# Loading the first input ahead of the key weights, and one burst for the second modulation

## The chip, the cores and the metric

The kernel runs on one core of a Trainium2 chip. The metric is device time in microseconds of one execution, the median of several runs. In the profile PE is TensorE's matmul side and PEld its weight loads, DVE is VectorE, ACT is ScalarE, POOL is GpSimd, and SP is SyncE, whose queue issues nearly all DMAs here.

## What is computed

Two post-norm layers run over 1024 latent tokens and 256 context tokens of width 1024. Each layer modulates its input with a shift and a scale made from a conditioning vector, projects it to queries, keys, values and a gate, attends (windowed attention with 16 query heads over 4 key heads in the first layer, neighbourhood attention in the second), gates, projects back and normalises. The part that matters here is the very start of layer one:

```python
shift, scale, gate = jnp.split(silu_c @ w_ada[i] + b_ada[i], 3, axis=-1)
shift_c, scale_c, gate_c = jnp.split(silu_cc @ w_ada[i] + b_ada[i], 3, axis=-1)
u = h * (1.0 + scale[:, None, :]) + shift[:, None, :]
uc = hc * (1.0 + scale_c) + shift_c
...
q, k, v, g = _split_a(u @ w_in)
```

## The kernel before

The width of 1024 is cut into eight slices of 128 rows, called kt. Tokens stand in the free dimension: 1280 of them, in chunks (CHUNKS) of 512, 512 and 256; the first two are latent tokens, the last is the context.

Products are made at high precision from two parts: a tile is copied by ACT to a rounded high part (L164 for weights, wh; L568 for inputs, uAh), and the difference from the original, made by DVE or POOL, is the low part (L166, wl; L569, uAl). One product is three matmuls: high by high, low weight by high input, high weight by low input (L578, L579, L580 for keys; L588 to L590 for values).

The first stage is a loop over kt from -1 to 8 (L594). Its pieces:

- `mod_load(kt)` (L518) issues DMAs: two tiles of modulation weights (wada, 512 KB each), the weights of the key and value projections that are due (wr, 256 KB each, by `w.load`), and the slice of the input (hraw, 640 KB, 1280 tokens).
- `mod_rows(kt)` (L527) multiplies the conditioning vectors with the modulation weights: 16 calls, 32 matmul instructions, into one half of the PSUM tile kc. For kt above 1 these stand in one burst: each call after the first is tied to the call emitted just before it on TensorE (`keep_in_program_order`). For kt 0 and 1 they are free, so that each half can run when its weights are there. ACT copies the result to rows (L544).
- `mod(kt)` (L546) sums the rows with one small matmul (L549) whose moving operand is sel, the last four columns of the tile bad, and adds the biases, other columns of bad, on DVE (L550). The result adc holds shift and scale.
- `u_make(kt)` (L557) applies scale and shift to the three chunks in place (ACT at L564 for the first chunk, DVE at L566 for the other two), and makes high and low parts.
- `k_mm(kt)` (L571) makes the key products of the slice, into kp for the latent tokens (512 wide) and kc for the context (256 wide), for two halves of the key columns (nt). `v_mm(kt)` (L582) makes the value products of the first 512 tokens.
- `w.split(n)` (L153) makes high and low parts of the weight tiles up to number n. Tiles 0, 1, 4 and 5 are key weights, 2, 3, 6 and 7 value weights.

Before the loop, 12 bf16 matmuls on zeros run (L475), and 12 more after the first modulation (L607).

What each engine does in what order is not the order of the text. A planner sets it when the program is built: it goes by the order of emission and by when it reckons that operands are ready, and then fixes one order for each engine; at run time each engine goes through its list strictly. DMAs are issued by SP in one such list. The tile bad is loaded second of all, behind cT, the conditioning vectors.

Of the kernel before, what the change touches and what calls it, by code (L numbers as in the profile page):

```python
# [15 lines left out]
ALU = mybir.AluOpType  # L16
# [14 lines left out]
CHUNKS = ((0, 512), (512, 512), (1024, 256))  # L31
# [12 lines left out]
def f32(ap):  # L44
    return ap.bitcast(F32)
# [37 lines left out]
def build(tc, i, out):  # L83
    nc = tc.nc
    mm = nc.tensor.matmul
    dma = nc.sync.dma_start
# [18 lines left out]
    cT = cp.tile([P, KT, 2], F32, name="cT")  # L105
    dma(cT, i["cT"])
    bad = cp.tile([P, 52], F32, name="bad")
    dma(bad, i["bada"])
    sel = bad[:, 48:52]
    lnc = cp.tile([P, 2, KT], F32, name="lnc")  # L110
    half = cp.tile([P, 1], F32, name="half")
# [25 lines left out]
    class Weights:  # L137
# [15 lines left out]
        def split(self, upto):  # L153
            while self.ns < min(upto, self.cap):
                j = self.ns
                self.load(j + 1)
                r = self.raw.pop(j)
                if j in VALUES:
                    t = pp.tile([P, 2, 512], F32R, tag="wada", bufs=10, name=f"wv{j}")
                    hi, lo = t[:, 0], t[:, 1]  # L160
                else:
                    hi = wp.tile([P, 512], F32R, tag="whi", bufs=4, name=f"wh{j}")
                    lo = wp.tile([P, 512], F32R, tag="wlo", bufs=4, name=f"wl{j}")
                nc.scalar.copy(hi, r)  # L164
                e = nc.vector if j < 8 or j >= NA and j % 2 else nc.gpsimd
                e.tensor_tensor(lo, r, f32(hi), ALU.subtract)  # L166
                self.got[j] = (hi, lo)
                self.ns += 1
# [14 lines left out]
    NA = len(srcs)  # L183
# [6 lines left out]
    w = Weights(srcs)  # L190
# [280 lines left out]
    def warm(out, n):  # L471
        for _ in range(n):
            mm(out, zero[:, 0:P], zero, start=True, stop=True)
# [2 lines left out]
    nc.scalar.activation(th0, cT, AF.Tanh, scale=0.5)  # L476
    nc.vector.scalar_tensor_tensor(th0, th0, 1.0, cT, ALU.add, ALU.mult)
    nc.vector.tensor_scalar(sil[:, :, 0:2], th0, 0.5, None, ALU.mult)
    nc.vector.tensor_scalar(bad[:, 8:16], bad[:, 8:16], 1.0, None, ALU.add)
    cos = ap_.tile([P, S], F32, name="cos")  # L480
    sin = ap_.tile([P, S], F32, name="sin")
    msk = ap_.tile([P, 1152], BF16, name="msk")
# [33 lines left out]
    raws, wada, rows = {}, {}, {}  # L516

    def mod_load(kt, upto):  # L518

        wada[kt] = [pp.tile([P, 4, 2 * P], F32, tag="wada", bufs=10, name="wada") for _ in range(2)]  # L520
        for hf in range(2):
            dma(wada[kt][hf], i["wadaC"][kt, hf])
        w.load(upto)
        raws[kt] = pp.tile([P, T], F32, tag="hraw", bufs=4, name="hraw")
        dma(raws[kt], i["hT"][:, kt, :])

    def mod_rows(kt):  # L527

        ws = wada.pop(kt)

        burst = kt > 1
        for n, hf in enumerate((1, 0) if burst else (0, 1)):
            for r in range(2):
                for x in range(2):
                    for kh in range(2):
                        g = 32 * (2 * x + kh)
                        ins = mm(
                            kc[g : g + 32, 512:640], sil[:, 4 * hf + 2 * r + kh, :], ws[hf][:, 2 * r + kh, x * P : (x + 1) * P],
                            start=n + r == 0, stop=n + r == 2, tile_position=(0, g),
                        )  # L540
                        if burst and n + r + x + kh:
                            tc.keep_in_program_order(ins)
        rows[kt] = pp.tile([P, P], F32, tag="rows", bufs=2, name="rows")
        nc.scalar.copy(rows[kt], kc[:, 512:640])  # L544

    def mod(kt):  # L546

        pa = kc[:, 768 + 4 * kt : 772 + 4 * kt]
        mm(pa, rows.pop(kt), sel, start=True, stop=True)  # L549
        nc.vector.tensor_tensor(  # L550
            adc[:, kt],
            pa.rearrange("p (x v) -> p x v", x=2),
            bad[:, kt : kt + 9 : 8].unsqueeze(2).to_broadcast([P, 2, 2]),
            ALU.add,
        )

    def u_make(kt):  # L557
        r = raws.pop(kt)
        for c, (t0, n) in enumerate(CHUNKS):
            v, tok = c // 2, slice(t0, t0 + n)  # L560
            x = r[:, tok]
            sc, sh = adc[:, kt, 1, v : v + 1], adc[:, kt, 0, v : v + 1]
            if c == 0:
                nc.scalar.activation(x, x, AF.Identity, bias=sh, scale=sc)  # L564
            else:
                nc.vector.tensor_scalar(x, x, sc, sh, ALU.mult, ALU.add)  # L566
            hi, lo = uA.at(kt, tok)
            nc.scalar.copy(hi, x)  # L568
            nc.vector.tensor_tensor(lo, x, f32(hi), ALU.subtract)  # L569

    def k_mm(kt):  # L571
        for c, (t0, n) in enumerate(CHUNKS):
            for nt in range(2):
                hi, lo = w.got[KEYS[2 * (kt // 4) + nt]]
                sl = slice((kt % 4) * P, (kt % 4 + 1) * P)
                rh, rl = uA.at(kt, slice(t0, t0 + n))
                pt = kps[c, nt] if c < 2 else kc[:, nt * C : nt * C + C]
                mm(pt, hi[:, sl], rh, start=kt == 0 and (c < 2 or nt == 0), stop=False)  # L578
                mm(pt, lo[:, sl], rh, start=False, stop=False)  # L579
                mm(pt, hi[:, sl], rl, start=False, stop=kt == KT - 1 and (c < 2 or nt == 1))  # L580

    def v_mm(kt):  # L582
        hi, lo = w.got[VALUES[kt // 2]]
        sl = slice((kt % 2) * 256, (kt % 2 + 1) * 256)
        for t in range(4):
            lh, ll = uA.at(kt, slice(t * P, (t + 1) * P))
            pt = vps[:, t * 256 : (t + 1) * 256]
            mm(pt, lh, hi[:, sl], start=kt == 0 and t % 2 == 0, stop=False)  # L588
            mm(pt, lh, lo[:, sl], start=False, stop=False)
            mm(pt, ll, hi[:, sl], start=False, stop=kt == KT - 1 and t % 2 == 1)  # L590


    upto = (2, 3, 4, 4, 6, 7, 8, 8)
    for kt in range(-1, KT + 1):  # L594
        if kt + 1 < KT:
            for n in range(3) if kt < 0 else (kt + 3,) if kt + 3 < KT else ():
                mod_load(n, upto[n])
                if n == 0:
                    w.split(2)
            mod_rows(kt + 1)  # L600
        if kt > 0:
            k_mm(kt - 1)
        if kt + 1 < KT:
            mod(kt + 1)
        if kt < 0:

            warm(vps[:, 0:512], 12)  # L607
        if kt > 0:
            v_mm(kt - 1)
        if kt < KT and kt >= 0:  # L610
            u_make(kt)
            w.split(upto[min(kt + 1, 7)])
    dma(ident, i["ident"])
    dma(lnc, i["lnc"])
# [168 lines left out]
    def att_steps(subs, qk, st, tr, pv, last_of_unit, costs, need, ahead, rise, split=False):  # L783

        seq = []
        n = len(subs)
        for k in range(-ahead, n + 2 + split):
            row = []

# [51 lines left out]
    for p in range(8):  # L841
# [6 lines left out]
        if p < 7:  # L848
            n = len(att)
# [323 lines left out]
    for n, row in enumerate(rowsB):  # L1173
        ex = []
        if n < len(subsB):
            h, jp, r = subsB[n]
# [65 lines left out]
    for b in range(8):  # L1242
        x = ob.tile([P, D], F32, tag="x", bufs=3, name="x")
# [129 lines left out]
```

## Time and profile before

| | |
|---|---|
| median of 3 runs | 1434.9 us |
| lowest and highest run | 1433.47 and 1436.19 us |
| the profiled execution | 1432.09 us, of which the span is 1430.3 us |
| first matmul of the first modulation (L537) | 5.63 us |
| first input's modulation begins (L564, L566) | 10.02 us |
| first key product (L578) | 11.94 us |
| first keys taken from PSUM (L494) | 58.85 us |

The span runs from the first to the last instruction of the profile; all times within are microseconds from its start. A row of the timeline has start, duration, engine, line, operation, output and inputs, count, and in brackets the idle time just before with what ended it. Weight loads overlap matmuls and matmuls overlap each other, so the distance between two starts says more than a duration.

### The profile page before, as it was taken

The page shows a single profiled execution, that of the slowest core. Times are in us where ns is not written, and L with a number is a line of the kernel's source. Part 1 is how long each engine was busy: PE and PEld are TensorE (multiplying, and loading weights), DVE is VectorE, ACT ScalarE, POOL GpSimd, SP SyncE. Part 2 cuts the span into 40 slices and gives each one's busy share as a digit, 9 for nine tenths or more (in the row PEclk, how much of TensorE's full clock was granted, in tenths as well). Part 3 has the DMA queues.
Part 4 walks back from the last instruction along what each step waited for, and adds up shares of the span by engine and source line. Part 5 has one row for each costly group of instructions (what it writes and reads, how often), then busy time and mean ns, then how long its engine had stood idle before and what let it go on. Part 6 is the DMA issues. An engine that isn't in the chain of part 4 may idle for free. (4 is left out here: it accounts for less than half of the span.)

```text
span 1430.3 us, 25152 instructions
## 1 busy us (share of the span) xinstructions
PE 1388.8 (97%) x8816; PEld 1215.8 (85%) x8816; DVE 978.4 (68%) x2214; ACT 732.1 (51%) x1559; POOL 631.2 (44%) x779
## 2 busy tenths in 40 slices
PE   8999999999999999999999999999999999998997
PEld 6988898888888888788898899888988899887876
DVE  4658887878878789566433765555665665667598
ACT  4337776676776778332222545545454454557300
POOL 0326676667666667233311333333233233336663
PEclk9999999999999999999999999999999999999999
DMA  9572114123222123444287575464655464476564
GB/s 367 182 229 85 57 53 129 48 79 101 70 71 63 56 80 121 133 132 133 71 258 219 156 202 166 141 173 145 176 150 170 141 192 147 120 206 199 140 162 133
DMA packets 127453, 202.39 MB, mean 141 GB/s; under 512 B 9696, under 2 KB 65376, under 8 KB 127328
## 3 DMA queue, kind: packets, MB, share of 16 engines
q1 hardware_dynamic: 127328, 200.79, 47.0%
q8 instruction: 70, 1.15, 0.3%
q14 instruction: 55, 0.45, 0.1%
HBM read 145.18 MB, written 55.57 MB: 140 GB/s over the span
## 5 line engine op out<-in xcount | busy, mean ns | idle before, releaser
L332 POOL TENSOR_SCALAR s_B<-s_B,rs_B 128x640 f32<-128x640 f32 (+1 forms) x128 | 102.5, 801 | 294.1 <-DVE rs_B L331 250.4
L210 PE MATMUL pj<-uBh,wh 128*128 128x512 f32 (+1 forms) x448 | 175.9, 393 | 0.0
L211 PE MATMUL pj<-uBl,wh 128*128 128x512 f32 (+1 forms) x448 | 170.1, 380 | 0.0
L212 PE MATMUL pj<-uBh,wl 128*128 128x512 f32 (+1 forms) x448 | 170.1, 380 | 0.0
L327 ACT ACTIVATE s_B<-s_B,m_B 128x640 f32<-128x640 f32 (+1 forms) x128 | 102.9, 804 | 129.5 <-DVE m_B L320 128.9
L327 ACT ACTIVATE s_A<-s_A,m_A 128x641 f32<-128x641 f32 (+2 forms) x160 | 119.5, 747 | 81.9 <-DVE m_A L320 59.2
L166 POOL TENSOR_TENSOR wl<-wr,wh 128x512 fp32r<-128x512 f32 x64 | 87.4, 1365 | 159.5 <-ACT wh L164 145.5
L332 POOL TENSOR_SCALAR s_A<-s_A,rs_A 128x640 f32<-128x640 f32 (+2 forms) x160 | 129.6, 810 | 63.6 <-DVE rs_A L331 57.4
L320 DVE CUSTOM_DVE_ANT_0 s_A<-S_A,msk,nsk 128x640 f32<-128x640 f32 (+2 forms) x160 | 123.6, 774 | 31.2 <-PE S_A L735 16.2
L210 PE MATMUL pj<-uAh,wh 128*128 128x512 f32 (+1 forms) x384 | 140.1, 365 | 0.8 <-DVE otmp L774 0.8
L211 PE MATMUL pj<-uAl,wh 128*128 128x512 f32 (+1 forms) x384 | 137.6, 358 | 0.0
L345 DVE TENSOR_TENSOR pt_B<-T_B,pt_B 128x640 fp32r<-128x640 f32 (+1 forms) x128 | 100.9, 788 | 53.4 <-ACT pt_B L343 52.9
L212 PE MATMUL pj<-uAh,wl 128*128 128x512 f32 (+1 forms) x384 | 137.2, 357 | 0.0
L345 DVE TENSOR_TENSOR ptl_A<-T_A,pth_A 128x640 fp32r<-128x640 f32 (+2 forms) x160 | 114.2, 713 | 14.8 <-PE pvA L763 7.3
L339 PE MATMUL T_A<-ident,s_A 128*128 128x128 f32 x672 | 100.9, 275 | 10.6 <-DVE m_A L320 4.5
L339 PEld LDWEIGHTS T_A<-ident,s_A 128*128 128x128 f32 x672 | 77.3, 140 | 37.4 <-POOL s_A L332 10.1
L320 DVE CUSTOM_DVE_ANT_0 s_B<-S_B,bias 128x640 f32<-128x640 f32 (+1 forms) x128 | 100.3, 784 | 10.1 <-PE S_B L1067 9.3
L343 ACT CAST pt_B<-T_B 128x640 fp32r<-128x640 f32 (+1 forms) x128 | 84.5, 660 | 41.0 <-PE T_B L339 40.1
L343 ACT CAST pth_A<-T_A 128x640 fp32r<-128x640 f32 (+2 forms) x160 | 96.4, 602 | 16.5 <-PE T_A L339 15.1
L212 PEld LDWEIGHTS pj<-uBh,wl 128*128 128x128 f32 x448 | 84.2, 188 | 16.6
L339 PE MATMUL T_B<-ident,s_B 128*128 128x128 f32 x608 | 88.6, 275 | 8.8 <-DVE m_B L320 4.5
L339 PEld LDWEIGHTS T_B<-ident,s_B 128*128 128x128 f32 x608 | 70.3, 141 | 27.1 <-issue 13.5
(221 smaller groups left out, 3887.7 us busy)
## 6 DMA issues: line engine op xcount, KB each, us to landing
kB<-kdB SPq DMA_DIRECT2D x64, 320.0 KB, 5.2
gw<-in_wadaT SPq DMA_DIRECT2D x48, 256.0 KB, 2.8
vdB<-st SPq DMA_DIRECT2D x20, 512.0 KB, 3.5
vB<-vdB SPq DMA_DIRECT2D x16, 640.0 KB, 4.6
wada<-in_wadaC SPq DMA_DIRECT2D x16, 512.0 KB, 9.6
kdB<-st SPq DMA_DIRECT2D x16, 512.0 KB, 2.9
qdB<-st SPq DMA_DIRECT2D x16, 512.0 KB, 3.6
qB<-qdB SPq DMA_DIRECT2D x32, 256.0 KB, 4.7
```

The costliest lines, as they stand in the source:

```text
L166: e.tensor_tensor(lo, r, f32(hi), ALU.subtract)
L210: mm(pt[:, :n], hi[:, sl], rh, start=kt == 0, stop=False)
L211: mm(pt[:, :n], hi[:, sl], rl, start=False, stop=False)
L212: mm(pt[:, :n], lo[:, sl], rh, start=False, stop=kt == KT - 1)
L320: nc.vector.tensor_tensor_reduce(outp, sc, in1, scale, init if init is not None else 3e38, ALU.add, ALU.min, accum_out=s.m)
L327: nc.scalar.activation(s.t[:, :n], s.t[:, :n], AF.Exp, bias=s.m, scale=-1.0, accum_out=s.sum)
L332: nc.gpsimd.tensor_scalar(s.t[:, : s.w], s.t[:, : s.w], s.rs, 1.0, ALU.mult, ALU.mult)
L339: nc.tensor.transpose(tp[:, k * P : (k + 1) * P], s.t[:, src * P : (src + 1) * P], ident)
L343: nc.scalar.copy(pt.hi[:, :n, hl, :], tv)
L345: nc.vector.tensor_tensor(pt.lo[:, :n, hl, :], tv, f32(pt.hi[:, :n, hl, :]), ALU.subtract)
```

## The change

Four things change, all in the first stage.

1. The DMA of bad and the addition of 1 to its scale columns move from the head of the program into `mod_load(0)`, behind the first input.
2. In `mod_load(0)` the first input's DMA is issued ahead of the two key weights.
3. For kt = 0, `u_make` and `w.split(2)` move to the head of the iteration: the first chunk is modulated first (now on DVE), then the two key weights are split, then the other two chunks are modulated (the context on POOL). The ACT copies of the two key weights are tied to the instruction emitted before them on ACT, and the low part of the second one goes from DVE to POOL.
4. The first chunk's six key matmuls are emitted ahead of the second modulation. The second modulation (kt = 1) becomes one burst too, all its calls tied, the first one to the last of these key matmuls. The other two chunks' key products stay where all of them stood.

```diff
@@ head @@
-    dma(bad, i["bada"])
...
-                nc.scalar.copy(hi, r)
-                e = nc.vector if j < 8 or j >= NA and j % 2 else nc.gpsimd
+                ins = nc.scalar.copy(hi, r)
+                if j < 2:
+                    tc.keep_in_program_order(ins)
+                e = nc.vector if j < 8 and j != 1 or j >= NA and j % 2 else nc.gpsimd
...
-    nc.vector.tensor_scalar(bad[:, 8:16], bad[:, 8:16], 1.0, None, ALU.add)
...
-        w.load(upto)
         raws[kt] = pp.tile([P, T], F32, tag="hraw", bufs=4, name="hraw")
+        if kt:
+            w.load(upto)
         dma(raws[kt], i["hT"][:, kt, :])
+        if kt == 0:
+            dma(bad, i["bada"])
+            nc.vector.tensor_scalar(bad[:, 8:16], bad[:, 8:16], 1.0, None, ALU.add)
+            w.load(upto)
...
-        burst = kt > 1
+        burst = kt > 0
...
-                        if burst and n + r + x + kh:
+                        if kt == 1 or burst and n + r + x + kh:
                             tc.keep_in_program_order(ins)
...
-    def u_make(kt):
-        r = raws.pop(kt)
-        for c, (t0, n) in enumerate(CHUNKS):
+    def u_make(kt, cs=(0, 1, 2)):
+        r = raws[kt]
+        for c in cs:
+            t0, n = CHUNKS[c]
...
-            if c == 0:
+            if c == 0 and kt:
                 nc.scalar.activation(x, x, AF.Identity, bias=sh, scale=sc)
+            elif c == 2 and not kt:
+                nc.gpsimd.tensor_scalar(x, x, sc, sh, ALU.mult, ALU.add)
             else:
                 nc.vector.tensor_scalar(x, x, sc, sh, ALU.mult, ALU.add)
...
     for kt in range(-1, KT + 1):
+        if kt == 0:
+            u_make(0, (0,))
+            w.split(2)
+            u_make(0, (1, 2))
+            k_mm(0, (0,))
         if kt + 1 < KT:
             for n in range(3) if kt < 0 else (kt + 3,) if kt + 3 < KT else ():
                 mod_load(n, upto[n])
-                if n == 0:
-                    w.split(2)
             mod_rows(kt + 1)
         if kt > 0:
-            k_mm(kt - 1)
+            k_mm(kt - 1, (0, 1, 2) if kt > 1 else (1, 2))
...
-            u_make(kt)
+            if kt:
+                u_make(kt)
             w.split(upto[min(kt + 1, 7)])
```

More of the change, by code (lines that the diff above doesn't have):

```diff
@@ L569, in u_make, with k_mm @@
             nc.vector.tensor_tensor(lo, x, f32(hi), ALU.subtract)
-    def k_mm(kt):
-        for c, (t0, n) in enumerate(CHUNKS):
+    def k_mm(kt, cs=(0, 1, 2)):
+        for c in cs:
+            t0, n = CHUNKS[c]
             for nt in range(2):
```

## The prediction

> **What bounds the kernel now.** I read the page's head and busy times first, then the windows of the first stage (busy time of PE, PEld, DVE, ACT, POOL with counts, granted clock, DMA share, GB/s).
>
> ```profile
> span 1430.3 us, 25152 instructions
> PE 1388.8 (97%) x8816; PEld 1215.8 (85%) x8816; DVE 978.4 (68%) x2214; ACT 732.1 (51%) x1559; POOL 631.2 (44%) x779
> ...
> 24.00:36.00 12.00, 12.00 (x128) 10.36 (x128) 7.62 (x17) 6.40 (x13) 0.00 (x0) 1.00 1.03 405
> 57.00:80.00 23.00, 23.00 (x184) 22.52 (x183) 15.79 (x23) 4.99 (x10) 10.63 (x7) 1.00 0.47 160
> ```
>
> TensorE is busy 97% of the span, and the change touches only the first stage. From 24 to 36 us, and again from 57 to 80, PE has no gap, although the DMA engines are still full (share 1.03). So a microsecond won on PE before 24 us should reach the end, and what is not won there cannot be won later by this change. Which PE work stands at the start, and what releases it, is in the timeline of PE (start, duration, line, operation):
>
> ```profile
> 7.99 0.39 PE L549 MATMUL kc<-bad,rows 128*128 128x4 f32 x2
> 8.23 1.67 PE L473 MATMUL vps<-zero 128*128 128x512 bf16 x7
> 11.36 0.65 PE L537 MATMUL kc<-wada,sil 128*32 128x128 f32 x16 [1.46 <-DMA wada<-in_wadaC]
> 11.94 0.50 PE L578 MATMUL kp<-uAh,wh 128*128 128x512 f32 x1
> 13.37 0.65 PE L537 MATMUL kc<-wada,sil 128*32 128x128 f32 x16
> 13.94 0.50 PE L580 MATMUL kp<-uAl,wh 128*128 128x512 f32 x1
> 16.41 0.50 PE L578 MATMUL kp<-uAh,wh 128*128 128x512 f32 x1 [0.34 <-ACT uAh L568]
> 18.67 1.08 PE L537 MATMUL kc<-wada,sil 128*32 128x128 f32 x32
> 20.25 0.28 PE L578 MATMUL kc<-uAh,wh 128*128 128x256 f32 x1
> 20.96 0.28 PE L549 MATMUL kc<-bad,rows 128*128 128x4 f32 x2
> 22.75 0.39 PE L589 MATMUL vps<-wv,uAh 128*128 128x256 f32 x1 [1.06 <-DVE wv L166]
> ```
>
> Three idle stretches: 1.46 us before 11.36, 0.34 before 16.41, 1.06 before 22.75. They are all that PE can win besides doing the same work denser: 2.9 us of 1432. Pitches: the six 256-wide key products from 20.25 to 20.96 give 0.12 each, so 0.24 for a 512-wide one; half a modulation takes 0.57 (13.37 to 13.94), and one in a single burst about 1.0 (the 1.08 of the row at 18.67, less the overlap of the last). The context's six 256-wide products of the first input stand at 20.25, behind products of the second input: the order on an engine is not the text's but is fixed when the program is built.
>
> **The transfers.** Issue times from the timeline of SP, time to landing from the DMA view of the stretch around each issue (KB, us to landing):
>
> ```profile
> 1.19 0.42 SPq L108 DMA_DIRECT2D bad<-in_bada  x1
> bad<-in_bada SPq DMA_DIRECT2D x1, 26.0 KB, 2.1
> 2.12 0.43 SPq L522 DMA_DIRECT2D wada<-in_wadaC  x1
> wada<-in_wadaC SPq DMA_DIRECT2D x1, 512.0 KB, 4.6
> 3.07 0.43 SPq L150 DMA_DIRECT2D wr<-in_wAk  x1
> wr<-in_wAk SPq DMA_DIRECT2D x1, 256.0 KB, 5.3
> 3.54 0.43 SPq L525 DMA_DIRECT2D hraw<-in_hT  x1
> hraw<-in_hT SPq DMA_DIRECT2D x1, 640.0 KB, 6.4
> 5.71 0.59 SPq L525 DMA_DIRECT2D hraw<-in_hT  x1
> hraw<-in_hT SPq DMA_DIRECT2D x1, 640.0 KB, 9.0
> 4.50 0.51 SPq L522 DMA_DIRECT2D wada<-in_wadaC  x1
> wada<-in_wadaC SPq DMA_DIRECT2D x1, 512.0 KB, 8.0
> 7.75 0.33 SPq L522 DMA_DIRECT2D wada<-in_wadaC  x1
> wada<-in_wadaC SPq DMA_DIRECT2D x1, 512.0 KB, 10.6
> ```
>
> Landings are issue plus wait: bad 3.3, first modulation weights whole 6.7, second key weight 8.4, first input 9.9, second modulation weights whole 12.5, second input 14.7, third modulation weights 18.35. They come in the order of issue. From 8.4 to 9.9 the 640 KB of the input took 1.57 us, 0.41 MB/us.
>
> In the changed kernel bad leaves the front: one issue slot, 1.19 to 1.65, so the weights land at about 6.25. The input no longer has 512 KB of key weights ahead: 512/0.41 = 1.28 us. First input: 9.94 - 1.28 - 0.46 = **8.2**. The key weights land 0.64 and 1.28 us behind it, at 8.9 and 9.5. Bad lands between 4.7 (issue near 2.6 plus its 2.1) and 9.5 (with the key weights); I take 8.2, right behind the input, because all the quoted landings keep the order; at 9.5 all below would be 1.3 later, the sum +0.8. [...] Everything behind this group has the same bytes ahead as before: the second modulation's weights still land at 12.5, the second input at 14.7. SP's later issues wait for earlier landings, and the third modulation's may now wait for the input at 8.2 instead of the weights at 6.7. I cost that at nothing: the transfer of 7.75 took 10.6 us to land, so the engines have several microseconds queued; without that cover it would be up to 1.5 us on the third input.
>
> **The first products.** Rows for the chain:
>
> ```profile
> 3.36 0.17 DVE L479 TENSOR_SCALAR bad<-bad 128x8 f32<-128x8 f32 x1 [2.21 <-DMA bad<-in_bada]
> 8.41 0.16 DVE L550 TENSOR_TENSOR adc<-kc,bad 128x4 f32<-128x4 f32 x1 [4.50 <-PE kc L549]
> 14.83 0.16 DVE L550 TENSOR_TENSOR adc<-kc,bad 128x4 f32<-128x4 f32 x1 [1.83 <-PE kc L549]
> 15.03 0.87 DVE L566 TENSOR_SCALAR hraw<-hraw,adc 128x512 f32<-128x512 f32 x2
> L166 POOL TENSOR_TENSOR wl<-wr,wh x12: 1288/1301/1744, 55.6 to 186.6; 128x512 fp32r<-128x512 f32 x12
> L164 ACT CAST wh<-wr x3: 615/618/622, 7.8 to 29.8; 128x512 fp32r<-128x512 f32 x3
> L332 POOL TENSOR_SCALAR s_A<-s_A,rs_A 128x256 f32<-128x256 f32 x32 | 21.4, 668 | 5.0 <-DVE rs_A L331 5.0
> 55.56 1.38 POOL L166 TENSOR_TENSOR wl<-wr,wh 128x512 fp32r<-128x512 f32 x1 [54.53 <-ACT wh L164]
> 55.71 1.26 DVE L618 TENSOR_SCALAR nsk<-nsk 128x16 f32<-128x16 f32 x1
> ```
>
> L549 needs bad (its last columns select the sums), so it moves from 7.99 to about 8.3, and the sums come 0.4 later (7.99 to 8.41), at 8.7. The warming matmuls behind it (1.67) end at about 10.2, in time. Modulation of the first 512 tokens starts at 8.9 (0.2 behind, as 14.83 to 15.03); DVE takes two thirds of the row's 0.87, 0.58. Then ACT makes the high part to 10.1, and only after it, because the copies are now tied to that place, the two weight casts of 0.62 each: 10.65 and 11.2 (before, both ran ahead of the input). The first key product can start near **10.7** instead of 11.94. DVE makes both low parts it owns (about 0.69 each) by 11.4. The second weight's low part is now POOL's: 1.30 from 11.2, done at 12.5, where DVE took 0.69. The last two first-token products wait for it, so the six end at 13.1, and the second modulation, now tied behind them in one burst, runs from 13.1 to 14.1 (its weights are there at 12.5). Its second half ended at 13.94 before, so its sums come about **0.2 later**, 15.0, and the second input's products start at 16.6 instead of 16.41 (its data are there at 14.7).
>
> What PE has done by then decides. Between 10.7 and 16.6 it has six products (1.4), the burst (1.0), the second 512 tokens (1.4), the context (0.7) and the small matmuls (0.3): 4.8 of 5.9 us, so everything of the first input can be finished. Before, the six context products, 6 x 0.12 = 0.7, were still owed at 16.41. **Sum: +0.2 - 0.7 = -0.5 us.** The burst's data for the third modulation are there at 18.35, behind which PE has 12 products of the second input (2.8) from 16.6 to 19.4, so that gate does not bite. The wait of 1.06 at 22.75 hangs on the third modulation's sums and the DVE work behind them; with six products fewer ahead of L549 (20.96) this moves earlier with the rest, and I leave its length as it is. POOL's share of the context's modulation, 0.67 by the nearest row, lies beside DVE's. Of the moves that cost nothing, the first add to bad (0.17) lies beside L549.
>
> **A rule against it.** The last two rows show a 16-wide DVE scalar operation taking 1.26 us while POOL makes a low part; an 8-wide one took 0.17 with POOL at rest. [...]
>
> **The rivals.**
> *Also the value wait goes (about -1.5 us, 1433.4).* The value weights' split, behind the modulation on DVE at present, may be placed ahead of it in the new order. For: SP's order puts these weights ahead of the second input, so they are there by 14.7; against: its place in the text is unchanged. -0.5 - 1.06 = -1.56.
> *Nothing (1434.9).* The 0.5 is eaten at one of the next gates (the third modulation's L549, at 20.96 in the old order), since PE only waits longer there; PE's idle time before 22.75 would grow to about 1.5.
> [...]
> *The order later.* The order being built anew, a shift at the start could reorder the attention stages. The longest single wait of PE that the waits view shows there is 2.9 us, and that is my bound for this, both ways.
>
> ```profile
> PE T_B L339 <- DVE m_B L320: 4.5, 5, 2.9
> ```
>
> **How the numbers follow.** The profiled execution is 1432.09 us (span 1430.3), 2.8 below the median 1434.9 of three runs between 1433.47 and 1436.19. The change is 0.5 us in either; against the median, **1434.4**. Chances: forecast 0.43, value wait gone 0.20, nothing 0.13, POOL slower 0.11, a reordered later stage 0.13. The range takes the unknowns of the start (from -1.9, the forecast with the waits of 1.06 and 0.34 gone too, to +1.3) and the scatter of the runs: below, the 1.4 from the median to the lowest run; above, half of the 1.3 to the highest, as that end is a rival of 0.11. So 1431.6 to 1436.8. A measurement of this kernel tells about 0.2% (2.9 us) from no change: only the later order, or the value wait with a good draw, passes that downwards (0.13), only the later order or POOL's rival with a bad draw upwards (0.07). Same: 0.80.
>
> **What would show it.** First input landed near 8.2; first key product near 10.7; second modulation one group of 32 near 13.1; context products of the first input before 16.6; PE at 24 us half a microsecond further. Wrong if bad lands after the key weights, if PE sits idle between 11.5 and 13 for more than a microsecond, or if the waits of PE after 80 us differ from before.

## The result, and the profile after

| | before | after |
|---|---|---|
| median of 22 runs each | 1435.48 us | 1440.38 us |
| lowest and highest run | 1430.16 and 1438.56 us | 1432.90 and 1445.02 us |
| the profiled execution, and its span | 1432.09, 1430.3 us | 1438.73, 1437.0 us |
| second modulation's sums (second adc of DVE) | 14.83 us | 18.50 us |
| first keys taken from PSUM | 58.85 us | 62.55 us |

The ratio after to before is 1.003, with a 95% interval of 1.002 to 1.004: the change costs 2.9 to 5.7 us. The forecast was 1434.4 us, half a microsecond faster, with a range up to 1436.8 and a chance of 0.80 that the two kernels could not be told apart.

TensorE's timeline of the changed kernel, first stage (start, duration, engine, line, operation, idle time just before and what ended it; L543 is the modulation, L555 its sum, L588 to L590 the products):

```profile
9.17 0.28 PE L555 MATMUL kc<-bad,rows 128*128 128x4 f32 x2
9.31 0.81 PE L475 MATMUL vps<-zero 128*128 128x512 bf16 x3
12.11 1.32 PE L588 MATMUL kp<-uAh,wh 128*128 128x512 f32 x2 [1.99 <-ACT wh L163]
13.23 0.63 PE L589 MATMUL kp<-uAh,wl 128*128 128x512 f32 x1
13.66 0.63 PE L590 MATMUL kp<-uAl,wh 128*128 128x512 f32 x1
...
16.29 0.40 PE L589 MATMUL kp<-uAh,wl 128*128 128x512 f32 x1
16.61 1.08 PE L543 MATMUL kc<-wada,sil 128*32 128x128 f32 x32
18.08 0.39 PE L555 MATMUL kc<-bad,rows 128*128 128x4 f32 x2
20.07 0.50 PE L588 MATMUL kp<-uAh,wh 128*128 128x512 f32 x1 [1.61 <-ACT uAh L577]
23.95 0.28 PE L588 MATMUL kc<-uAh,wh 128*128 128x256 f32 x1
26.45 0.38 PE L599 MATMUL vps<-wv,uAh 128*128 128x256 f32 x1 [1.05 <-DVE wv L168]
```

Four things differ from the forecast. The first product starts at 12.11, where 11.94 was before and 10.7 was forecast. The products behind it stand 0.43 us apart (13.23 to 13.66), where a pitch of 0.24 was taken. The burst of the second modulation starts at 16.61, where 13.1 was forecast: eleven products stand ahead of it and not six. And the second input's first product starts at 20.07 instead of 16.41, behind an idle stretch of 1.61 us instead of 0.34. The wait for the value weights, 1.05, is unchanged, and the context's products of the first input, at 23.95, still stand behind the second input's.

The other engines' timelines in the same stretch:

```profile
8.62 0.17 DVE L530 TENSOR_SCALAR bad<-bad 128x8 f32<-128x8 f32 x1 [5.36 <-DMA bad<-in_bada]
9.49 0.16 DVE L556 TENSOR_TENSOR adc<-kc,bad 128x4 f32<-128x4 f32 x1 [0.70 <-PE kc L555]
9.77 0.81 POOL L573 TENSOR_SCALAR hraw<-hraw,adc 128x256 f32<-128x256 f32 x1 [8.74 <-DVE adc L556]
10.61 0.93 ACT L577 CAST uAh<-hraw 128x256 fp32r<-128x256 f32 x2 [2.78 <-POOL hraw L573]
11.44 1.14 ACT L163 CAST wh<-wr 128x512 fp32r<-128x512 f32 x2
12.66 1.34 POOL L168 TENSOR_TENSOR wl<-wr,wh 128x512 fp32r<-128x512 f32 x1 [2.08 <-ACT wh L163]
13.13 1.42 DVE L578 TENSOR_TENSOR uAl<-hraw,uAh 128x512 fp32r<-128x512 f32 x1 [0.27 <-ACT uAh L577]
18.50 0.16 DVE L556 TENSOR_TENSOR adc<-kc,bad 128x4 f32<-128x4 f32 x1 [3.95 <-PE kc L555]
62.55 0.73 DVE L495 STREAM_SHUFFLE rb<-kp 128x512 f32<-128x512 f32 x1
```

ACT is seen to sit idle for 2.78 us until POOL has modulated the context; the context's cast goes first in ACT's list, the first tokens' cast second (both in the row at 10.61), and only then, from 11.44, come the two key weights. Before, these two casts ran from 7.83 to 8.98, in the wait for the input, and cost nothing. Loading the input first has put them behind it.

The windows of the changed kernel show the clock (the third figure from the end is the granted clock of TensorE):

```profile
11.00:12.00 1.00, 0.00 (x0) 0.00 (x0) 0.85 (x2) 1.00 (x4) 0.00 (x0) 1.00 1.06 418
12.00:13.00 1.00, 0.89 (x2) 0.56 (x3) 0.86 (x2) 1.00 (x3) 0.34 (x1) 0.62 1.02 414
13.00:14.00 1.00, 1.00 (x3) 0.54 (x2) 0.87 (x1) 0.10 (x1) 1.00 (x1) 0.50 1.04 418
14.00:15.00 1.00, 1.00 (x3) 0.83 (x3) 0.55 (x1) 0.00 (x0) 0.00 (x1) 0.50 1.02 406
15.00:16.00 1.00, 1.00 (x4) 0.78 (x3) 0.00 (x0) 0.00 (x0) 0.00 (x0) 0.67 0.99 389
...
1394.00:1398.00 4.00, 4.00 (x11) 3.15 (x12) 3.49 (x6) 0.00 (x0) 1.19 (x2) 0.58 0.73 195
```

After PE's idle stretch of 1.99 us the clock is half for about 3.4 us, just while the first products run. In the kernel before it was 1.00 in each of these windows.

**Where the time went.** The two profiles differ by 6.7 us of span: 3.7 at the first keys (58.85 to 62.55), and 3.0 behind them. The 3.7 stay as a nearly constant lag: the first attention scores start at 100.9 instead of 97.2, the second layer's at 786.5 instead of 783.0 (3.5), and the last of these at 1335.7 instead of 1331.5 (4.2). The last 2.5 come in the tail, where the changed kernel's profile has half clock in the last row above, and the kernel before 1.00 in the same stretch. Such windows come and go: the profiles of the experiments below have none to four of them behind the first keys, and with that 1369.4 us (e14_value, mean granted clock 0.999) to 1379.5 us (e1_warm20, 0.993) from there to the end. So the loss at the first keys is the change's, but for what the start adds (next paragraph); of the 4.9 between the medians the other 1.2 lie within the interval. The profiles of kernels made from the changed one have one to four of these windows, those made from the kernel before none to two (mean granted clocks of 0.993 to 0.997 and 0.996 to 0.999); whether the change has a part in that is open.

**What one profile can show.** The 12 matmuls ahead of the loop are the same in every kernel, and still they take between 4.10 and 5.30 us (e14_value, and e7_wl1_dve_warm and e16_value_warm), so that the first modulation begins anywhere from 5.24 to 6.44. The first row is from the kernel before, the second from the changed one:

```profile
1.21 4.50 PE L473 MATMUL warm<-zero 128*128 128x512 bf16 x12 [1.21 <-DVE zero L469]
1.21 4.82 PE L475 MATMUL warm<-zero 128*128 128x512 bf16 x12 [1.21 <-DVE zero L471]
```

The first modulation began at 5.63 and 5.96. In the kernel before nothing hangs on this: the input and the second weights come later. In the changed kernel the chain from the first modulation to the first product has no slack, so up to 0.3 of its 3.7 can be this start and not the change. Each kernel below was profiled once; a difference of a few tenths between two of them shows little.

### The profile page after: what moved, and what is told of

It reads as the page before. It is cut to its first block, busy times and chain, and to the rows that moved or that the text cites. A ratio compares the mean times of both kernels' runs of the same rounds, so it can differ in the third digit from the quotient of the medians.

```text
span 1437.0 us, 25153 instructions
## 1 busy us (share of the span) xinstructions
PE 1391.9 (97%) x8816; PEld 1218.5 (85%) x8816; DVE 980.0 (68%) x2213; ACT 731.6 (51%) x1558; POOL 634.5 (44%) x781
## 3 DMA queue, kind: packets, MB, share of 16 engines
q8 instruction: 70, 1.15, 0.3%
## 5 line engine op out<-in xcount | busy, mean ns | idle before, releaser
L329 ACT ACTIVATE s_A<-s_A,m_A 128x641 f32<-128x641 f32 (+2 forms) x160 | 119.6, 748 | 81.6 <-DVE m_A L322 58.9
L334 POOL TENSOR_SCALAR s_A<-s_A,rs_A 128x640 f32<-128x640 f32 (+2 forms) x160 | 129.8, 811 | 62.4 <-DVE rs_A L333 55.9
L347 DVE TENSOR_TENSOR pt_B<-T_B,pt_B 128x640 fp32r<-128x640 f32 (+1 forms) x128 | 100.9, 788 | 53.6 <-ACT pt_B L345 53.2
```

What stands on the lines that cost most here:

```text
L329: nc.scalar.activation(s.t[:, :n], s.t[:, :n], AF.Exp, bias=s.m, scale=-1.0, accum_out=s.sum)
L334: nc.gpsimd.tensor_scalar(s.t[:, : s.w], s.t[:, : s.w], s.rs, 1.0, ALU.mult, ALU.mult)
L347: nc.vector.tensor_tensor(pt.lo[:, :n, hl, :], tv, f32(pt.hi[:, :n, hl, :]), ALU.subtract)
```

## The experiments

Two times tell the kernels apart within one profile: the second modulation's sums, and the first keys taken from PSUM, which end the first stage. Theory: the second input's products can't start before the second modulation's sums, so the first keys follow these sums one for one, and the loss of 3.7 is made of whatever delays the sums. Rivals: the loss is in the transfers; in POOL's share; in the wait for the value weights; or in the half clock alone. All kernels, times in us; sums and first keys are from one profile each, the time is a median of 10 to 12 runs (22 for the changed kernel, one run where no interval stands), and the ratio is against runs of the kernel before on the same chip:

| kernel | sums | first keys | difference | time | ratio (95%) |
|---|---|---|---|---|---|
| before | 14.83 | 58.85 | 44.02 | | |
| after | 18.50 | 62.55 | 44.05 | 1440.38 | 1.003 (1.002 to 1.004) |
| e1_warm20 | 17.53 | 61.56 | 44.03 | 1436.18 | 1.0015 (1.000 to 1.003) |
| e5_behind | 18.58 | 62.72 | 44.14 | 1439.16 | 1.002 (1.0006 to 1.0035) |
| e9_first_warm | 15.50 | 59.61 | 44.11 | 1436.55 | 1.000 (0.9984 to 1.0016) |
| e2_free_warm | 17.45 | 61.45 | 44.00 | 1435.38 | |
| e7_wl1_dve_warm | 17.58 | 61.62 | 44.04 | 1437.83 | |
| e6_c2_dve | 17.18 | 62.70 | 45.52 | 1437.22 | |
| e4_code_only | 19.45 | 63.48 | 44.03 | 1438.47 | 1.0026 (1.001 to 1.0042) |
| e3_dma_only | 15.66 | 59.68 | 44.02 | 1437.49 | 1.0017 (1.0004 to 1.0031) |
| e11_bad_front | 15.96 | 60.00 | 44.04 | 1435.31 | 1.000 (0.9985 to 1.0014) |
| e13_burst_only | 15.59 | 59.64 | 44.05 | 1434.54 | |
| e14_value | 15.04 | 57.74 | 42.70 | 1434.58 | 0.9989 (0.9972 to 1.0006) |
| e16_value_warm | 15.40 | 58.13 | 42.73 | 1433.11 | 0.9982 (0.9965 to 0.9998) |

The difference is 44.0 to 44.1 in all but three kernels, although the sums move by 4.6 us: the theory holds, and the sums are what has to be explained. The exceptions are told below.

**Is it the half clock? e1_warm20.** More warming matmuls ahead of the first products:

```diff
-            warm(vps[:, 0:512], 12)
+            warm(vps[:, 0:512], 20)
```

> The changed kernel with 20 instead of 12 warming matmuls behind the first modulation, so that TensorE has work until the first key product. Mark: the first time that keys are taken from PSUM (58.85 us in the kernel before, 62.55 in the changed one, +3.7). Theory: the +3.7 is three terms, a later start of the first product (+0.75), 3.4 us at half clock behind an idle stretch of 2.0 us (+1.7), and a longer wait for the second modulation (+1.27). Then no half clock shows near 12 to 16 us and the mark is near 60.9, the time 1.5 to 2 us below the changed kernel's. Rival, the second modulation's place alone sets the mark: the clock is full but PE only waits longer, mark 62.3 or more.

The timeline of PE in this kernel:

```profile
12.11 1.02 PE L588 MATMUL kp<-uAh,wh 128*128 128x512 f32 x2 [0.27 <-ACT wh L163]
14.06 0.50 PE L589 MATMUL kp<-uAh,wl 128*128 128x512 f32 x1 [0.40 <-POOL wl L168]
15.63 1.08 PE L543 MATMUL kc<-wada,sil 128*32 128x128 f32 x32
19.11 0.50 PE L588 MATMUL kp<-uAh,wh 128*128 128x512 f32 x1 [1.61 <-ACT uAh L577]
```

The first product starts at the same 12.11, now behind an idle stretch of 0.27, and the granted clock is 1.00 in each window from 9 to 21 us. The sums come 0.97 earlier, the first keys 0.99. So the half clock is about 1.0 of the 3.7, where 1.7 was expected of it, and 2.7 are left at full clock; the first keys lie between what the theory (60.9) and its rival (62.3 or more) had said. The wait for POOL's low part, which half clock had covered, now shows: 0.40.

**Is it the place of the second modulation? e5_behind.** The products of the second 512 tokens are held behind the burst (with True, `k_mm` ties the first matmul of each product):

```diff
             mod_rows(kt + 1)
+            if kt == 0:
+                k_mm(0, (1,), True)
...
-            k_mm(kt - 1, (0, 1, 2) if kt > 1 else (1, 2))
+            k_mm(kt - 1, (0, 1, 2) if kt > 1 else (2,))
```

> The changed kernel with the second 512 tokens' key products tied behind the second modulation's burst, so that the burst follows the six first-token products at once; nothing else. Theory: the burst starts near 15.1 instead of 16.6, the second input's products 1.3 to 1.5 us earlier, mark (first keys taken from PSUM) 61.1 to 61.3; half clock stays. Rival, the clock alone costs the time: the mark stays at 62.3 to 62.6.

The burst came earlier, at 15.46, but took 1.39 where 1.08 is its length at full clock, so part of it, by this estimate, was under half clock, and the matmul that sums it went behind the six products that were tied to the burst, to 18.27. The sums are no earlier, 18.58, and neither are the first keys, 62.72 against the 61.1 to 61.3 expected and the 62.3 to 62.6 of the rival. The run moves the burst without moving what matters, and so tells only that the burst by itself isn't the gate; its sums are.

**e9_first_warm.** The burst stands ahead of the first tokens' products too, and 22 warming matmuls are there to keep the clock up:

```diff
-                        if kt == 1 or burst and n + r + x + kh:
+                        if burst and n + r + x + kh:
...
-            k_mm(0, (0,))
...
             mod_rows(kt + 1)
+            if kt == 0:
+                k_mm(0, (0,), True)
...
-            warm(vps[:, 0:512], 12)
+            warm(vps[:, 0:512], 22)
```

> The changed kernel with the second modulation's burst put ahead of the first-token products (these are tied behind it instead of the other way round, in the order of the text) and 22 warming matmuls, so that TensorE is never idle long enough to lose its clock. Transfers, casts and POOL's share stay as changed. Theory, the harm is the late second modulation plus the clock: burst near 12.5 (when its weights land), its sums near 14.8, the second input's products near 16.3, no half clock at the start, mark (first keys taken from PSUM) 58.6 to 59.6, as in the kernel before (58.85). Rival, the late first products are harm in themselves: mark above 60.3.

```profile
12.68 1.08 PE L543 MATMUL kc<-wada,sil 128*32 128x128 f32 x32 [0.72 <-DVE wl L168]
13.69 0.50 PE L588 MATMUL kp<-uAh,wh 128*128 128x512 f32 x1
...
15.19 0.28 PE L555 MATMUL kc<-bad,rows 128*128 128x4 f32 x2
```

Its timeline shows the first product at 13.69, 1.6 us later than in the changed kernel, and still the sums come at 15.50, 3.0 earlier, and the first keys 2.9 earlier. An early first product was worth nothing; an early second modulation is worth its full shift. The burst took 1.08 and the products 0.50 or less, as in e1_warm20 at full clock; against that run the place is worth 17.53 - 15.50 = 2.0. The other 0.67 is seen in the rows too. ACT copies the result of the burst for the summing matmul; this copy and the summing matmul stand so in the kernel before (the first two rows), and the copy so in the changed kernel, in e1_warm20 and in e9_first_warm:

```profile
14.08 0.27 ACT L544 COPY rows<-kc 128x128 f32<-128x128 f32 x1 [1.91 <-PE kc L537]
14.51 0.28 PE L549 MATMUL kc<-bad,rows 128*128 128x4 f32 x2
17.76 0.27 ACT L550 COPY rows<-kc 128x128 f32<-128x128 f32 x1 [4.66 <-PE kc L543]
16.78 0.27 ACT L550 COPY rows<-kc 128x128 f32<-128x128 f32 x1 [3.68 <-PE kc L543]
13.82 0.27 ACT L550 COPY rows<-kc 128x128 f32<-128x128 f32 x1 [1.03 <-PE kc L543]
```

At the copy the changed kernel is 3.7 late and e1_warm20 2.7, and e9_first_warm is 0.26 early, although its burst could begin only at 12.68, when all of its weights were there (they land at 12.5). So the place is worth the whole 2.7 there, up to 0.3 of it by the earlier start of that profile (5.42 against 5.96). Then e9_first_warm loses again: its summing matmul, ready at 14.09, stands at 15.19 behind six products, 1.10 later, where the kernel before has 0.16. An order with it right behind the burst wasn't tried.

**Is it the tie, or the burst? e2_free_warm and e13_burst_only.** The first unties the second modulation in the changed kernel, with 20 warming matmuls (to be held against e1_warm20); the second makes one burst of it in the kernel before and changes nothing else:

```diff
# e2_free_warm, in the changed kernel
-        burst = kt > 0
+        burst = kt > 1
...
-                        if kt == 1 or burst and n + r + x + kh:
+                        if burst and n + r + x + kh:
# e13_burst_only, in the kernel before
-        burst = kt > 1
+        burst = kt > 0
```

> The changed kernel with the second modulation free of all ties, in two halves as before, and 20 warming matmuls; to be compared with the run that has the warming alone (second modulation's sums at 17.53, mark 61.56). Law to be tested here and below: mark = 58.85 + (sums of the second modulation - 14.83). Theory, not the burst but the place behind the first-token products costs the time: the halves fall behind six and eight products, sums 17.2 to 17.6, mark 61.2 to 61.7. Rival, the burst is the harm: sums before 16.3, mark below 60.4.

> The kernel before with the second modulation as one burst, not tied to the first-token products, nothing else. By the same law: no half of it can go ahead of the products any more; in the program's order it stands behind the six first-token products, from about 13.5, sums 15.0 to 15.6, mark 59.0 to 59.6. Rival, a burst saves the gaps of two halves: mark 58.5 to 58.85.

Untied, the second modulation ran in halves at 14.76 and 15.99, and the sums came at 17.45, 0.08 from e1_warm20: tied or not, the planner puts it late here. In it and in e1_warm20 the text emits the six first products ahead of it; in e9_first_warm, where the text has it ahead of them, it came early. In the kernel before, the burst alone costs 0.8 (sums +0.76, first keys +0.79), as its timeline shows: the half that ran at 11.36 now waits for its other half, and six products get ahead of it. It is the place again, then, that costs; the input landed 0.2 later in this profile, which is in the 0.8 too.

```profile
12.09 0.50 PE L578 MATMUL kp<-uAh,wh 128*128 128x512 f32 x1 [2.36 <-ACT uAh L568]
...
13.70 1.08 PE L537 MATMUL kc<-wada,sil 128*32 128x128 f32 x32
```

**Is it the transfers? e3_dma_only, e4_code_only and e11_bad_front.** The first has only the new order of the DMAs (input, bad, key weights), the second everything but that, and the third, in the kernel before, the input ahead of the key weights with bad left at the head:

```diff
# e3_dma_only, in the kernel before
-    dma(bad, i["bada"])
-    nc.vector.tensor_scalar(bad[:, 8:16], bad[:, 8:16], 1.0, None, ALU.add)
...
-        w.load(upto)
         raws[kt] = pp.tile([P, T], F32, tag="hraw", bufs=4, name="hraw")
+        if kt:
+            w.load(upto)
         dma(raws[kt], i["hT"][:, kt, :])
+        if kt == 0:
+            dma(bad, i["bada"])
+            nc.vector.tensor_scalar(bad[:, 8:16], bad[:, 8:16], 1.0, None, ALU.add)
+            w.load(upto)
# e4_code_only: the same lines taken back in the changed kernel
# e11_bad_front, in the kernel before
-        w.load(upto)
         raws[kt] = pp.tile([P, T], F32, tag="hraw", bufs=4, name="hraw")
+        if kt:
+            w.load(upto)
         dma(raws[kt], i["hT"][:, kt, :])
+        if kt == 0:
+            w.load(upto)
```

> The kernel before with only the new order of the DMAs (first input ahead of the key weights, bad behind it, its addition moved along). Theory, the code's order and not the transfers' does the harm: the first input's modulation starts near 9.7 (gated by bad), the first product near 12, the second modulation is free to go between, mark 58.3 to 59.3 against 58.85. Rival, bad's late landing is the harm: mark above 60.

> The changed kernel with the old order of the DMAs (bad second, key weights ahead of the first input). Theory, the code's order does the harm: the first input lands at 9.9, the first product comes near 12.4, the second modulation is tied behind it, TensorE is idle for about 2.5 us before it and falls to half clock; mark 60.5 to 62.5. Rival, the transfers' order does the harm: mark below 59.3.

> The kernel before with the first input's DMA ahead of the key weights and nothing else: bad stays second in the queue. Beside the earlier run with the transfers' order alone (mark 59.68) it shows what bad's late landing costs. Theory, bad gates the first modulation there: now it starts near 8.7, first product near 10.7, mark 58.2 to 58.9. Rival, the key weights' casts, which now stand behind the input on ACT, eat the gain: mark 59.2 to 59.7.

ACT's and PE's timelines of e3_dma_only:

```profile
9.19 0.81 ACT L567 ACTIVATE hraw<-hraw,adc 128x512 f32<-128x512 f32 x1 [2.01 <-DVE adc L553]
9.90 1.12 ACT L163 CAST wh<-wr 128x512 fp32r<-128x512 f32 x2
10.93 1.44 ACT L571 CAST uAh<-hraw 128x512 fp32r<-128x512 f32 x3
```

```profile
11.60 0.50 PE L581 MATMUL kp<-uAh,wh 128*128 128x512 f32 x1 [1.98 <-ACT uAh L571]
11.94 0.40 PE L582 MATMUL kp<-uAh,wl 128*128 128x512 f32 x1
12.26 0.65 PE L540 MATMUL kc<-wada,sil 128*32 128x128 f32 x16
```

ACT modulates at 9.19 instead of 10.02, and then spends 1.03 us on the two weight casts that were done by 8.98 before. The first product comes only 0.34 earlier for 0.83 of earlier modulation, and now two products stand ahead of the second modulation's first half, which goes from 11.36 to 12.26. The first keys come 0.83 later. With bad at the head (e11_bad_front) the input is used at 9.19 as well, when it has landed, the first half goes to 12.79 and the first keys come 1.15 later. So the new order of the transfers, alone, brings the input forward and loses, with bad late or not. Of the two, e3_dma_only had been expected at 58.3 to 59.3 (its rival: above 60) and e11_bad_front at 58.2 to 58.9 (its rival: 59.2 to 59.7); 59.68 and 60.00 came, later than the theory in both. The code alone loses most, 4.63 (63.48, above the 60.5 to 62.5 expected), with the sums at 19.45: its first product waits 3.71 us for the later input, and the half clock then falls on the burst (1.90 us long; the granted clock is 0.53, 0.50, 0.50 and 0.77 in the windows from 15 to 19 us). With both the loss is 3.70. The parts don't add up, as each alone is planned anew: each half of the change makes the second modulation late on PE, and with the new code the new transfers take some of the loss back.

**Is it POOL? e6_c2_dve and e7_wl1_dve_warm.** The first gives the context's modulation back to DVE, the second the second key weight's low part, with 20 warming matmuls:

```diff
# e6_c2_dve
-            elif c == 2 and not kt:
-                nc.gpsimd.tensor_scalar(x, x, sc, sh, ALU.mult, ALU.add)
# e7_wl1_dve_warm
-                e = nc.vector if j < 8 and j != 1 or j >= NA and j % 2 else nc.gpsimd
+                e = nc.vector if j < 8 or j >= NA and j % 2 else nc.gpsimd
...
-            warm(vps[:, 0:512], 12)
+            warm(vps[:, 0:512], 20)
```

> The changed kernel with the context's share of the first modulation back on DVE. Theory, the wait for POOL puts the context's cast ahead of the first tokens' on ACT and delays the first product by about 0.6: first product near 11.5 instead of 12.1, second modulation near 16.0, mark 61.7 to 62.1, or near 60.3 if the shorter idle stretch also spares the half clock. Rival, POOL's share lies beside other work: mark 62.4 to 62.7.

> The changed kernel with the second key weight's low part back on DVE, and 20 warming matmuls; beside the run with the warming alone (0.40 us of TensorE's time waits for POOL's low part there; sums 17.53, mark 61.56). Theory, POOL's low part costs no more than this wait: sums 17.0 to 17.3 and one fewer product ahead of the burst at most another 0.25 earlier, mark 60.8 to 61.35. Rival, DVE's queue gets longer by as much: mark 61.5 or more.

In e6_c2_dve ACT makes the first tokens' high part first (10.32), the first product starts at 11.52 behind only 1.34 of idle, and the early half clock is gone (0.39 and 0.40 for the products from 12.67 to 14.97, but for 0.50 behind a wait): sums at 17.18. But the windows show it 7 us later, behind the next wait of 1.61:

```profile
19.00:20.00 1.00, 1.00 (x4) 0.76 (x4) 1.00 (x3) 0.52 (x2) 0.00 (x0) 0.59 0.98 387
20.00:21.00 1.00, 1.00 (x4) 0.81 (x3) 0.35 (x2) 0.00 (x0) 0.00 (x0) 0.50 1.02 409
21.00:22.00 1.00, 1.00 (x4) 0.67 (x3) 0.00 (x0) 0.00 (x0) 0.00 (x0) 0.50 1.05 428
```

That is the exception with 45.52: 1.5 us lost behind the sums. The first keys, 62.70, came where the rival had them (62.4 to 62.7), but not for its reason: the first product was earlier as the theory had it, and the half clock moved. Against e1_warm20, also at full clock so far, the context on POOL is worth 0.35 at the sums (17.53 to 17.18). In e7_wl1_dve_warm the whole start of the profile lies 0.70 later (first product at 12.81 instead of e1_warm20's 12.11), by 0.5 already at the first modulation, behind the 12 matmuls ahead of the loop, which the edit doesn't touch; and the sums are no earlier than there, 17.58. They missed the window expected for them, and the first keys came as its rival had it; taken from the first product on, sums come 17.58 - 12.81 = 4.77 behind it, where e1_warm20 has 5.42. So POOL's low part is worth some 0.65 against the same on DVE, if the late start is taken out like this; one profile of each stands behind it, and the sums themselves didn't move.

**What might have been a gain: e14_value and e16_value_warm.** The only long wait in the kernel before that lies behind the sums is the 1.06 for the value weights' low part. Here two instructions of the third modulation (the copy of its rows on ACT, its sums on DVE) are tied to the instruction emitted before them, so that the split of the value weights goes first:

```diff
-        nc.scalar.copy(rows[kt], kc[:, 512:640])
+        ins = nc.scalar.copy(rows[kt], kc[:, 512:640])
+        if kt == 2:
+            tc.keep_in_program_order(ins)
...
-        nc.vector.tensor_tensor(
+        ins = nc.vector.tensor_tensor(
             adc[:, kt],
...
+        if kt == 2:
+            tc.keep_in_program_order(ins)
# e16_value_warm, besides
-            warm(vps[:, 0:512], 12)
+            warm(vps[:, 0:512], 17)
```

> The kernel before with the first value weight's split placed earlier on ACT and DVE: the third modulation's copy on ACT and its addition on DVE are tied behind it. Its data land near 13.2. Theory, the wait of 1.06 us of the value products ends there, and nothing later takes it up: mark 57.7 to 58.0, time about 1 us below the kernel before. Rival, the wait moves to another place: mark 58.6 to 58.9.

> The kernel before with the first value weight's split placed earlier (mark 57.74 in the run with that alone) and 17 instead of 12 warming matmuls behind the first modulation, so that the idle stretch ahead of the second modulation goes and can't cost clock in any run. Theory: mark 57.6 to 57.9 as without the warming, no half clock before 60 us, median 1 to 2 us below the kernel before. Rival, the warming gets in the way of the second modulation: mark above 58.2.

```profile
18.14 0.68 DVE L166 TENSOR_TENSOR wv<-wr,wv 128x512 fp32r<-128x512 f32 x1
```

The low part of the first value weight moves from 22.01 to 18.14, the wait is gone, and the first keys come at 57.74, 1.1 earlier than before, although the sums were 0.2 later. More warming on top of it bought nothing that shows: the second sums came 0.36 later and the first keys 0.39, outside of what was expected for them (57.6 to 57.9). This isn't all the warming's doing: the first modulation began at 6.44 instead of 5.24, behind the same 12 matmuls ahead of the loop, its sums came at 9.41 instead of 8.05, and the added matmuls stood behind that. The times are 0.11% and 0.18% below the kernel before; only the interval of e16_value_warm (0.9965 to 0.9998) lies wholly below 1, and just so. What both share is the tie, which is worth 1.3 us behind the sums (44.0 to 42.7).

## Why the prediction was wrong, step by step

**What bounds the kernel: right.** The first stage's loss reaches the later stages, 3.7 at the first keys, 3.7 at the first scores and 3.5 at the second layer's.

**The transfers: right.** The DMA view and SP's timeline of the changed kernel:

```profile
2.12 0.43 SPq L527 DMA_DIRECT2D hraw<-in_hT  x1
hraw<-in_hT SPq DMA_DIRECT2D x1, 640.0 KB, 6.2
2.60 0.43 SPq L529 DMA_DIRECT2D bad<-in_bada  x1
bad<-in_bada SPq DMA_DIRECT2D x1, 26.0 KB, 6.0
```

The input landed at 2.12 + 6.2 = 8.3 (forecast 8.2), bad at 8.6, behind it in order of issue. That is the order that the forecast had taken. The third modulation's weights were issued from 8.38 instead of 6.71, as the forecast had feared, and landed by 17.4, so the nothing that it put on this was right.

**The first products: 1.4 late.** Forecast 10.7, measured 12.11. Two steps make it up. The first modulation starts at 9.69 (DVE, 0.20 behind the sums at 9.49) and not at 8.9:

```profile
7.43 1.90 PE L475 MATMUL vps<-zero 128*128 128x512 bf16 x8
9.69 1.17 DVE L575 TENSOR_SCALAR hraw<-hraw,adc 128x512 f32<-128x512 f32 x2
```

Bad came 0.4 later than taken, but that didn't end last: the summing matmul started only at 9.17, behind eight warming matmuls that the forecast had behind it, when bad (8.6) and the addition to it (8.62 to 8.79, costed at nothing) were done. The rest, 0.6, is ACT's order: the forecast had the first tokens' high part and then the weights, but the context's cast, which waits for POOL, went first. POOL's 0.81 for the context, forecast to lie beside DVE's work for nothing, was on the path; in e6_c2_dve, without it, the first product came 0.59 earlier.

**The half clock: not foreseen.** The forecast let the warming matmuls end at 10.2 "in time" for a product at 10.7. The product came at 12.11, behind an idle stretch of 1.99, and the clock was 0.50 from 12.2 to 15.7. Worth 1.0 (e1_warm20).

**The second modulation: the step that failed.** "The six end at 13.1, and the second modulation, now tied behind them in one burst, runs from 13.1 to 14.1", with sums "0.2 later". A tie says what comes behind what; it does not say that nothing else comes between. The planner put five products of the second 512 tokens in between (four in e1_warm20), and the burst came at 16.61, 3.5 behind the forecast: 1.4 by the later first product, 1.0 by the half clock (15.63 in e1_warm20), and the rest, 1.1, nearly all by these products. The sums came at 18.50 instead of 15.0. Against the kernel before, 1.0 of the loss of 3.7 is the half clock (e1_warm20) and the other 2.7 is the place of the burst behind the products (up to 0.3 of it can be the later start): with the burst ahead of them (e9_first_warm) ACT's copy behind it came 0.26 earlier than in the kernel before. The burst as such cost nothing there. The 0.67 that e9_first_warm still lost is the place of its summing matmul, and the 0.8 of e13_burst_only is six products that got ahead of the burst.

**The credit of 0.7: never came.** The context's products were to be finished ahead of the second input's. The forecast asked only whether PE had time for them; it had said itself that the order on an engine isn't the text's, and the text too had left these products where they stood. They stand at 23.95, behind the second input's first ones, in the planner's order; PE instead sat idle for 1.61. In the kernel before, the changed one and e9_first_warm, PE does the same twelve products ahead of the second input's first one, and that is why the first keys follow the sums so exactly. Whether finishing the context there would be worth its 0.7 was not tried.

**The rivals.** POOL's low part, with its 0.11 the one rival on the right side, was a small part of the loss and not its cause. No run shows the +1.3 that the range has for it: the low part took 1.34, near the 1.30 that the forecast itself had charged and not the 1.74 of the longest before; at full clock 0.40 of waiting shows for it, and about 0.65 in all against the same on DVE. DVE felt it: the low part of the second 512 tokens took 1.42 beside it (the row at 13.13), and 0.69 in e7_wl1_dve_warm, where POOL was at rest. No wait of PE is seen to hang on this in e1_warm20. The value wait did not go (1.05), and no later stage was reordered to show in the lag.

## What to carry to other kernels

Before a transfer is moved ahead of another, ask what work ran in the wait that it shortens: here 1.15 us of weight casts were free, and became the path. Judge an early start by the next gate that the path must pass, not by the work that it lets finish: here the gate was the second modulation's sums, and all that was put ahead of them was loss. A tie in the order fixes a sequence and not a position, so whatever else a planner may put in between belongs in the forecast.

## What the hardware showed that was not expected

TensorE's clock fell to half after an idle stretch of 1.99 us (in the changed kernel and in e5_behind, and of 3.71 in e4_code_only), and of 1.61 in e6_c2_dve, but not after the same 1.61 in e1_warm20, 1.98 in e3_dma_only, the same 1.99 in e14_value, 2.26 in e11_bad_front or 2.36 in e13_burst_only. The fall is in the windows of the changed kernel (0.62, 0.50, 0.50 and 0.67 from 12 to 16 us), of e4_code_only (from 15 to 19) and of e6_c2_dve (from 19 to 23, the last of them 0.70); in e5_behind it is told from the products, 0.63 to 0.78 each from 13.47 to 14.90, and 0.40 or less from 17.11. In e1_warm20 the windows have 1.00; in the other four the products behind the stretch took 0.39 to 0.50, as in the kernel before at 1.00. Once down the clock stayed so for about 3.4 us, worked out from the windows of the three kernels, although PE was busy by then: in the changed kernel it did warming matmuls up to 10.12 and products from 12.11, and the half clock began at about 12.2. So the length of one idle stretch does not decide. What does, these runs do not show.

A like window in the tail, at 1394 to 1398 us in the changed kernel's profile, goes with about 3 us of time from the first keys to the end. Since such windows come in some executions and not in others, one execution says little about a change of this size, and the time of the first keys, within one profile, says much more, down to the few tenths by which the start itself differs.
